# Second mixer of a two-layer decoder trunk: sums of squares of k read from the diagonal of k's product with itself instead of from transposed copies of k

## The chip, the cores and the metric

The kernel runs on 1 core of one Trainium2 chip. The metric is the device time of one execution in microseconds (us), as the median of several runs. In the profile, PE is the matmul engine (TensorE) and PEld its weight loads, DVE is VectorE, ACT is ScalarE, POOL is GpSimd and SP is the engine from whose queue most of the DMAs are issued.

## What is computed

A trunk of two layers on 512 positions of 1024 channels in float32. Layer 0 has gated linear attention as mixer, layer 1 a gated DeltaNet; each is followed by a ConvFFN, and every sublayer ends in a LayerNorm. The change lies in the DeltaNet, with 8 heads of 128 channels:

```python
def l2_normalize(x):
    return x * lax.rsqrt(jnp.sum(jnp.square(x), -1, keepdims=True) + RMS_EPS)

def gdn_mixer(x, w_in, conv_w, a_log, dt_bias, norm_w, w_out):
    proj = x @ w_in
    ...
    qkv = jax.nn.silu(causal_dwconv(qkv, conv_w))
    q, k, v = jnp.split(qkv.astype(jnp.float32), [hk, 2 * hk], axis=-1)
    qc = l2_normalize(to_head_chunks(q, GDN_HEADS, GDN_CHUNK)) * GDN_DK ** -0.5
    kc = l2_normalize(to_head_chunks(k, GDN_HEADS, GDN_CHUNK))
    ...
    o = rms_norm(gdn_chunked(qc, kc, vc, beta, gc), norm_w)
    o = from_head_chunks(o).astype(x.dtype)
    return (o * jax.nn.silu(gate)) @ w_out

def gdn_chunked(q, k, v, beta, g):
    ...
    k_beta = k * beta[..., None]
    m = jnp.where(strict, jnp.einsum('bhnik,bhnjk->bhnij', k_beta, k) * decay_ij, 0.0)
    rhs = jnp.concatenate([v * beta[..., None], k_beta * jnp.exp(bcum)[..., None]], axis=-1)
    sol = lax.linalg.triangular_solve(m, rhs, left_side=True, lower=True, unit_diagonal=True)
    ...
```

So each position's k is divided by its length, for which its sum of squares is needed, and the products of all pairs of k in a chunk, scaled by beta and a decay, form a triangular matrix that is inverted. The kernel works with blocks of 128 positions, four to a sequence, and leaves k as it comes from the convolution; the lengths enter as factors.

## The kernel before

The program is unrolled. A Python planner writes the instructions in one order, from a clock of its own (`self.clk`) that every planned matmul advances: a matmul of 128 columns in full float32 by 0.224, a transposition by 0.11, one of the wide ones (512 columns) by 0.23. Side work is written as generators that are resumed between the wide matmuls when they fall due (`spawn` with a delay, `yield` with a pause, `until` and `set` for flags). PE therefore carries out the side products at fixed places among the wide matmuls, each engine takes its instructions in the order of the program, and a late input stalls the engine at that place. The wide matmuls are the projections: `fm` (a head's channels on the partitions), then `tm` (positions on the partitions) for the gates and the output. Each fm item takes 24 wide matmuls with a split weight (high and low part, `wh` from ACT, `wl` from DVE). Four weight buffers (`WB = 4`) rotate, and when the planner takes up an item it writes the split of the item two places further on (`LOOKAHEAD = 2`).

The DeltaNet's items come in this order: k of 8 heads with the columns for beta and the decay after the fourth (`ba_done`), v of 8 heads, q of 8 heads, then the gates. `gdn_conv` takes a head's result out of PSUM (ACT, then three DVE operations, then silu on ACT).

What stands around the change:

- `squares(which, hd)` transposes a pair of heads of k or q (four 128x128 transpositions a head, tile `qkT`, one PSUM bank a head) and lets ACT square each block with an accumulator output into `ssq`.
- `k_task(hd)` is started for both heads of a pair 6.0 after the second one's conversion. It calls `squares` for the pair, waits for the flag `dt` of its head (decays ready), makes the factors `bp` and `bn` on DVE from `ssq` and beta, multiplies k with itself on PE (tile `pg`), and lets DVE scale and mask this product out of PSUM into the slot `am`. Then DMAs on the POOL and SP queues write the 32x32 diagonal blocks of `am` to DRAM (`dblk`).
- `decays` fills the tiles `dt`: 8 broadcast DMAs on POOL, transpositions (`bat`) of the tile that DVE's scan writes, DVE differences, ACT exponentials. It is started by `ba_done` and sets `dt` of head n at its end plus 0.6 n + 1.0.
- `norms(1, rk)` waits for `ssq` of all heads and makes the factors with which `v_task` scales v.
- `base` waits for `am` of all heads, loads `dblk` as `m`, inverts the 32x32 blocks with 62 dependent DVE operations, writes the result to DRAM and loads it back as `T` and `rm` for four pairs of heads. For every pair it starts `inverse`, `INV_DELAY` later by the planner's clock: four blocks of small PE products (tiles V and R) with copies on ACT and DVE between them, which build the full inverse `rm`.
- `chain(g)`, for each half of the heads, needs v, `rm` and the masked products of q and k; it runs the recurrence over the four blocks, and its last flag is `r2`. `finish` then scales the gates by the outputs, and `split_y` transposes them (`yT`) for the output projection.

SBUF slots of 128x512 float32 come from a pool of 45 in this stage (`SLOTS`), and PSUM has 8 banks.

Of the kernel before, what the change touches and what calls it, by code (L numbers as in the profile page):

```python
# [12 lines left out]
AF = mybir.ActivationFunctionType  # L13
ALU = mybir.AluOpType
# [28 lines left out]
LOOKAHEAD = 2  # L43
TAIL = 4
HEADSTART = 4
INV_DELAY = 27.0
CONV_DELAY = 6.0
COLS_DELAY = 64.0
BASE_PACE = 1.8
# [3 lines left out]
def c4(t):  # L53
    return t.rearrange("p (c i) -> p c i", c=4)


def blk(i, n=P):
    return slice(i * n, i * n + n)


class Trunk:
# [85 lines left out]
    def keep(self, shape, s, dt=F32):  # L147
        return self.cp.tile(shape, dt, name=self.uid(s), tag=s)
# [1093 lines left out]
    def gdn(self, li, g, b):  # L1242
        nc = self.nc
# [8 lines left out]
        bn, bp, rk = keep("gd_bn"), keep("gd_bp"), keep("gd_rk")  # L1252
        ssq, rr = self.own([P, 2, DH, 4], "gd_ssq"), self.own([P, DH, 4], "gd_rr")
# [3 lines left out]
        q, k, v, am, rm, pj = ([None] * DH for _ in range(6))  # L1257
# [51 lines left out]
            self.set("decays", 1.0)  # L1309


        def squares(which, hd):

            for i in (hd, hd + 1):
                pt = self.psum("qkT")
                self.tr4(pt, (q, k)[which][i])
                for ck in range(4):
                    nc.scalar.activation(pt[:, blk(ck)], pt[:, blk(ck)], AF.Square,
                                         accum_out=ssq[:, which, i, ck:ck + 1])
                self.set(("ssq", which, i))  # L1320

        def k_done(ps, hd):
            k[hd] = self.gdn_conv(ps, 8 + hd, self.resid("conv"))
            if hd % 2:
                self.spawn(k_task(hd - 1), CONV_DELAY)
                self.spawn(k_task(hd), CONV_DELAY)

        def q_done(ps, hd):
            q[hd] = self.gdn_conv(ps, hd, self.slot("conv"))
            if hd % 2:  # L1330
                self.spawn(q_task(hd - 1), CONV_DELAY)

        def k_task(hd):
            t = k[hd]
            if hd % 2 == 0:
                squares(1, hd)
            yield from self.until(("dt", hd))
            nc.vector.tensor_scalar_add(bp[:, hd, :], ssq[:, 1, hd, :], RMS_EPS)
            nc.vector.reciprocal(bp[:, hd, :], bp[:, hd, :])
            nc.vector.tensor_mul(bp[:, hd, :], bp[:, hd, :], beta(hd))  # L1340
            nc.vector.tensor_scalar_mul(bn[:, hd, :], bp[:, hd, :], -1.0)
            yield 0.5
            pg = self.psum("pg")
            self.mm4(pg, t, t)
            am[hd] = a = self.slot("am")
            for ck in range(4):
                nc.vector.scalar_tensor_tensor(a[:, blk(ck)], pg[:, blk(ck)], bn[:, hd, ck:ck + 1],
                                               pj[hd][:, blk(ck)], ALU.mult, ALU.mult)
            for qq in range(4):
                r = blk(qq, 32)  # L1350
                u = hd // 4 * 64 + qq * 16 + hd % 4 * 4
                (nc.gpsimd, nc.sync)[qq % 2].dma_start(self.dblk[u:u + 4].rearrange("c j i -> j c i"), c4(a)[r, :, r])
            self.set(("am", hd), 2.0)

        def q_task(hd):
            squares(0, hd)
            for i in (hd, hd + 1):
                yield from self.until(("am", i))
            for i in (hd, hd + 1):
                pq = self.psum("pq")  # L1360
                self.mm4(pq, k[i], q[i])
                nc.vector.tensor_mul(pj[i], pj[i], pq)

                nc.gpsimd.affine_select(c4(pj[i]), c4(pj[i]), pattern=[[0, 4], [1, P]], compare_op=ALU.is_ge,
                                        fill=0.0, base=0, channel_multiplier=-1)
                self.set(("pj", i), 2.0)
# [9 lines left out]
        def base():  # L1376
# [17 lines left out]
            for pair in range(4):  # L1394
# [6 lines left out]
                for qq in range(4):  # L1401
# [5 lines left out]
                    for i in range(2):  # L1407
                        (nc.sync, nc.gpsimd)[qq % 2].dma_start(
                            c4(rm[2 * pair + i])[rw, :, rw],
                            self.dinv[u + 4 * i:u + 4 * i + 4].rearrange("c j i -> j c i"))  # L1410
                self.spawn(inverse(pair, t8), INV_DELAY)
                yield 4.5
# [271 lines left out]
```

## Time and profile before

| | before |
|---|---|
| median of 3 runs | 1256.84 us (1256.22 to 1257.76) |
| the profiled execution | 1261.5 us, its span 1259.8 us |
| DeltaNet up to the last gate projection | about 586 to 851 us of the span |
| PE busy in the span | 1242.6 us |
| DVE busy in the span | 914.2 us |
| ACT busy in the span | 584.2 us |
| granted TensorE clock, mean | 0.997 |

A line of the groups reads: program line, engine, operation, output <- inputs, shape and count, then busy time, mean duration, and the idle time of the engine ahead of them. In the table by stretches each engine's busy time stands with the number of its instructions. The chain of waits follows the last instruction back to what released it, piece by piece.

### The profile page before, as it was taken

To read this page: it belongs to the slowest core of one execution; us is meant where nothing else is said; L and a number is where in the kernel's file an instruction comes from. 1 tells how busy PE (TensorE), PEld (TensorE's weight loads), DVE (VectorE), ACT (ScalarE), POOL (GpSimd) and SP (SyncE) were. 2 spreads that over 40 slices of the span, in tenths; PEclk is the share of its full clock that TensorE was granted. 3 is DMA by queue.
4 is the path that set the end of the run, shared out by engine and by line. 5 is a ranking of instruction groups with operands and counts; after the bars stand their busy time and mean duration, and the time that the engine had idled before them with its cause. 6 is when DMAs were issued, how large, how long until landed. Compare 5 with 4: busy or idle time off the path is not lost.

```text
span 1259.8 us, 17201 instructions
## 1 busy us (share of the span) xinstructions
PE 1242.6 (99%) x6574; PEld 1050.7 (83%) x6574; DVE 914.2 (73%) x1541; ACT 584.2 (46%) x1062; POOL 115.1 (9%) x152
## 2 busy tenths in 40 slices
PE   9999999999999999989999999999999999999997
PEld 8878888988888888879888888988988878888886
DVE  4953556689957895765689955579588966796667
ACT  4644434634434443454765544544554434443440
POOL 4000000071000000001013030010044000000000
PEclk9999999999999999999999999999999999999999
DMA  7422224342453114441344341134443173323321
GB/s 206 117 67 67 67 84 134 134 134 67 130 154 100 61 57 117 122 132 51 101 138 117 109 103 41 62 124 118 144 134 101 34 217 93 92 71 113 100 68 67
DMA packets 169410, 130.72 MB, mean 104 GB/s; under 512 B 16232, under 2 KB 139946, under 8 KB 169328
## 3 DMA queue, kind: packets, MB, share of 16 engines
q1 hardware_dynamic: 164240, 120.47, 32.2%
q0 software_dynamic: 3888, 8.50, 2.2%
q8 instruction: 51, 0.84, 0.3%
q10 hardware_dynamic: 1200, 0.66, 0.2%
q14 instruction: 31, 0.25, 0.1%
HBM read 123.82 MB, written 5.78 MB: 103 GB/s over the span
## 4 chain that ended last, share of the span: by engine, by line
PE 87%; DVE 8%; ACT 2%; DMA 2%; issue 1%; SPq 0%; DVEq 0%; ACTq 0%
PE fm L193 44%; PE tm L193 22%; PE fold L193 11%; DVE wl L571 2%; PE o L193 2%; PE xT L210 1%; DMA raw<-in_gdn_w_in_dram 1%; PE R L193 1%; DVE conv L842 1%; DVE form L842 1%; PE V L193 1%; PE qkT L210 1%; PE vn L193 1%; PE pq L193 1%; PE pg L193 1%
## 5 line engine op out<-in xcount | busy, mean ns | idle before, releaser
L193 PE MATMUL fm<-xh,wh 128*128 128x512 f32 (+2 forms) x1104 | 402.5, 367 | 0.7 <-ACT xh L571 0.7
L193 PE MATMUL fm<-xl,wh 128*128 128x512 f32 (+2 forms) x1104 | 399.9, 365 | 0.0
L193 PE MATMUL fm<-xh,wl 128*128 128x512 f32 (+1 forms) x1088 | 395.9, 366 | 0.0
L571 DVE TENSOR_TENSOR wl<-raw,wh 128x1024 fp32r<-128x1024 f32 (+1 forms) x162 | 203.0, 1255 | 195.8 <-ACT wh L571 195.6
L571 ACT CAST wh<-raw 128x1024 fp32r<-128x1024 f32 (+1 forms) x162 | 169.5, 1046 | 259.2 <-PE fm L193 155.2
L193 PEld LDWEIGHTS fm<-xh,wh 128*128 128x128 f32 (+1 forms) x1104 | 206.9, 188 | 33.8 <-ACT xh L571 0.9
L193 PEld LDWEIGHTS fm<-xl,wh 128*128 128x128 f32 (+1 forms) x1104 | 207.0, 188 | 32.7 <-DVE xl L571 0.2
L193 PEld LDWEIGHTS fm<-xh,wl 128*128 128x128 f32 x1088 | 204.2, 189 | 33.3
L193 PE MATMUL fold<-wl,fh 128*128 128x512 f32 x224 | 87.4, 390 | 1.1 <-DVE wl L571 1.1
L193 PE MATMUL fold<-wh,fh 128*128 128x512 f32 x224 | 87.6, 391 | 0.0
L193 PE MATMUL fold<-wh,fl 128*128 128x512 f32 x224 | 87.2, 389 | 0.0
L842 DVE SCALAR_TENSOR_TENSOR conv<-fm,ffn_cw,conv 128x511 f32<-128x511 f32 x112 | 83.4, 745 | 5.1 <-ACT conv L840 3.7
L193 PE MATMUL tm<-wh,xh 128*128 128x512 f32 x192 | 78.5, 409 | 0.8 <-ACT qk L1043 0.8
L571 ACT CAST wh<-b 128x1024 fp32r<-128x1024 f32 x48 | 49.6, 1053 | 59.1 <-PE fold L193 25.8
L193 PE MATMUL tm<-wh,xl 128*128 128x512 f32 x192 | 75.2, 391 | 0.0
L193 PE MATMUL tm<-wl,xh 128*128 128x512 f32 x192 | 74.9, 390 | 0.0
L860 ACT ACTIVATE conv<-conv 128x512 f32<-128x512 f32 x44 | 27.8, 632 | 81.0 <-DVE conv L842 81.0
L571 DVE TENSOR_TENSOR wl<-b,wh 128x1024 fp32r<-128x1024 f32 x48 | 57.8, 1216 | 2.3 <-ACT wh L571 2.3
L769 POOL TENSOR_TENSOR h<-h,gb 128x512 f32<-128x512 f32 x16 | 28.1, 1778 | 329.3 <-DMA gb<-in_ln_g_dram 329.3
L1237 DVE SCALAR_TENSOR_TENSOR conv<-fm,gdn_cw,conv 128x509 f32<-128x509 f32 (+2 forms) x72 | 53.2, 743 | 1.8 <-ACT conv L1235 1.0
L193 PEld LDWEIGHTS fold<-wl,fh 128*128 128x128 f32 x224 | 42.0, 188 | 10.5 <-DVE wl L571 1.9
L193 PEld LDWEIGHTS fold<-wh,fh 128*128 128x128 f32 x224 | 42.0, 188 | 9.8 <-DVE h L931 1.2
(318 smaller groups left out, 1844.4 us busy)
## 6 DMA issues: line engine op xcount, KB each, us to landing
raw<-in_ffn_w_in_dram SPq DMA_DIRECT2D x88, 512.0 KB, 3.8
raw<-in_gdn_w_in_dram SPq DMA_DIRECT2D x32, 512.0 KB, 4.1
raw<-in_ffn_w_out_dram SPq DMA_DIRECT2D x28, 512.0 KB, 3.7
b<-in_ffn_w_out_dram SPq DMA_DIRECT2D x24, 512.0 KB, 4.9
raw<-in_gla_w_in_dram SPq DMA_DIRECT2D x23, 512.0 KB, 3.7
raw<-in_gla_w_out_dram SPq DMA_DIRECT2D x8, 512.0 KB, 3.7
raw<-in_gdn_w_out_dram SPq DMA_DIRECT2D x8, 512.0 KB, 3.9
h<-in_x_dram SPq DMA_DIRECT2D x8, 256.0 KB, 5.9
```

The source lines that it names most:

```text
L193: t = self.nc.tensor.matmul(out, a, b, start=start, stop=stop, skip_group_check=joined)
L210: t = self.nc.tensor.transpose(out, a, self.ident[:n, :n])
L571: return self.nc.scalar.copy(dst_h, src), self.nc.vector.tensor_sub(dst_l, src, dst_h)
L769: nc.gpsimd.tensor_mul(h[hf], h[hf], gb[hf])
L842: nc.vector.scalar_tensor_tensor(a[:, d:], ps[:, :S - d], tap(2 - d), a[:, d:], ALU.mult, ALU.add)
L860: nc.scalar.activation(a, a, AF.Gelu)
L1237: self.conv = nc.vector.scalar_tensor_tensor(a[:, d:], ps[:, :S - d], tap(3 - d), a[:, d:], ALU.mult, ALU.add)
```

## The change

The transpositions of k and their squares on ACT go. The product of k with itself is made at the place where they stood, before the wait for `dt`. ACT copies it into the slot `am`. DVE then multiplies each of its four blocks in PSUM by the identity, in place, with a sum over the row as a second output: the diagonal, which is the sum of squares, goes to `ssq`. The pause of 0.5 behind the factors goes. The scaling and masking reads the copy in SBUF and writes it in place. `squares` serves q alone. The delay of `inverse` goes from 27 to 35.

```diff
-INV_DELAY = 27.0
+INV_DELAY = 35.0
...
-        def squares(which, hd):
+        def squares(hd):
 
             for i in (hd, hd + 1):
-                pt = self.psum("qkT")
-                self.tr4(pt, (q, k)[which][i])
+                pt = self.psum("qT")
+                self.tr4(pt, q[i])
                 for ck in range(4):
-                    nc.scalar.activation(pt[:, blk(ck)], pt[:, blk(ck)], AF.Square,
-                                         accum_out=ssq[:, which, i, ck:ck + 1])
-                self.set(("ssq", which, i))
+                    nc.scalar.activation(pt[:, blk(ck)], pt[:, blk(ck)], AF.Square, accum_out=ssq[:, 0, i, ck:ck + 1])
+                self.set(("ssq", 0, i))
...
         def k_task(hd):
             t = k[hd]
-            if hd % 2 == 0:
-                squares(1, hd)
+            pg = self.psum("pg")
+            self.mm4(pg, t, t)
+            am[hd] = a = self.slot("am")
+            nc.scalar.copy(a, pg)
+            for ck in range(4):
+                nc.vector.tensor_tensor_reduce(pg[:, blk(ck)], pg[:, blk(ck)], self.ident, 1.0, 0.0,
+                                               ALU.mult, ALU.add, ssq[:, 1, hd, ck:ck + 1])
+            self.set(("ssq", 1, hd))
             yield from self.until(("dt", hd))
             nc.vector.tensor_scalar_add(bp[:, hd, :], ssq[:, 1, hd, :], RMS_EPS)
             nc.vector.reciprocal(bp[:, hd, :], bp[:, hd, :])
             nc.vector.tensor_mul(bp[:, hd, :], bp[:, hd, :], beta(hd))
             nc.vector.tensor_scalar_mul(bn[:, hd, :], bp[:, hd, :], -1.0)
-            yield 0.5
-            pg = self.psum("pg")
-            self.mm4(pg, t, t)
-            am[hd] = a = self.slot("am")
             for ck in range(4):
-                nc.vector.scalar_tensor_tensor(a[:, blk(ck)], pg[:, blk(ck)], bn[:, hd, ck:ck + 1],
+                nc.vector.scalar_tensor_tensor(a[:, blk(ck)], a[:, blk(ck)], bn[:, hd, ck:ck + 1],
                                                pj[hd][:, blk(ck)], ALU.mult, ALU.mult)
...
         def q_task(hd):
-            squares(0, hd)
+            squares(hd)
```

## The prediction

> **What bounds the kernel now.** I read the page first: busy shares and the chain of waits.
>
> ```profile
> span 1259.8 us, 17201 instructions
> PE 1242.6 (99%) x6574; PEld 1050.7 (83%) x6574; DVE 914.2 (73%) x1541; ACT 584.2 (46%) x1062; POOL 115.1 (9%) x152
> PE 87%; DVE 8%; ACT 2%; DMA 2%; issue 1%; SPq 0%; DVEq 0%; ACTq 0%
> ```
>
> PE is never free for long, and 87% of the chain is PE. A microsecond taken from PE's list shortens the kernel by one, unless an input is then late. So I need the slack of the others around the edit: the busy times by stretches (columns: length; PE, PEld, DVE, ACT, POOL busy with counts; clock; DMA share; GB/s).
>
> ```profile
> 615.00:625.00 10.00, 10.00 (x50) 8.28 (x49) 4.76 (x12) 8.85 (x25) 0.00 (x0) 1.00 0.40 105
> 625.00:635.00 10.00, 9.60 (x45) 7.67 (x44) 9.34 (x21) 4.88 (x7) 3.45 (x7) 1.00 0.45 123
> 635.00:645.00 10.00, 10.00 (x50) 8.38 (x49) 7.30 (x16) 6.26 (x22) 1.35 (x3) 1.00 0.78 256
> 645.00:660.00 15.00, 15.00 (x81) 12.79 (x80) 14.85 (x63) 9.19 (x25) 0.00 (x0) 1.00 0.23 65
> 660.00:680.00 20.00, 20.00 (x118) 17.60 (x118) 17.78 (x54) 13.37 (x26) 11.93 (x24) 1.00 0.50 124
> 680.00:722.50 42.50, 42.50 (x213) 35.79 (x212) 41.16 (x91) 24.24 (x61) 2.91 (x6) 1.00 0.34 94
> ```
>
> PE is full in all but one stretch. DVE is nearly full from 645 to 722.5 (14.85 of 15, 17.78 of 20, 41.16 of 42.5), where it scales `am` and runs `base`. It has room only in 615 to 625 (5.24 idle) and 635 to 645 (2.70). The edit takes work from PE and gives work to DVE just ahead of DVE's full stretch; that is the whole question.
>
> **The change part by part.** (1) PE. The pieces of the chain of waits (start, length, what):
>
> ```profile
> 611.27 0.87 PE qkT L210 x8
> ...
> 616.25 0.94 PE qkT L210 x8
> ...
> 635.96 0.87 PE qkT L210 x8
> ...
> 647.74 0.87 PE qkT L210 x8
> ...
> 664.03 2.68 PE pg L193 x24
> ```
>
> The four `qkT` pieces are k's, two heads each; they go: 0.87 + 0.94 + 0.87 + 0.87 = **3.55 us** off PE. The products, 2.68 for three heads, so 0.89 a head and 7.1 in all, stay at the same price, but move to where the transpositions were.
>
> (2) ACT. It loses 32 squares with their accumulator reads and gains 8 copies of a full bank; the nearest row for a copy is the cast of `yT`.
>
> ```profile
> L1318 ACT ACTIVATE qkT<-qkT 128x128 f32<-128x128 f32 x64 | 16.7, 261 | 1.5 <-PE qkT L210 1.0
> L1318 ACT ACTIVATION_READ_ACCUMULATOR qkT<-qkT 128x1 f32 x64 | 11.9, 186 | 0.0
> L571 ACT CAST yh<-yT 128x512 fp32r<-128x512 f32 x8 | 4.3, 622 | 4.5 <-PE yT L210 4.3
> ```
>
> That is 32 x (0.261 + 0.186) = 14.3 us of durations against 8 x 0.622 = 5.0. ACT gets lighter behind a full PE: nothing on the path.
>
> (3) DVE. It gains 32 multiplications by the identity with a row sum, out of and into PSUM. No operation of DVE here writes PSUM or has an accumulator, so the price is bounded by the nearest rows: the scaling of `am` out of PSUM, and ACT's accumulator read above.
>
> ```profile
> L1347 DVE SCALAR_TENSOR_TENSOR am<-pg,gd_bn,dt 128x128 f32<-128x128 f32 x32 | 9.2, 342 | 0.0
> L1587 DVE SCALAR_TENSOR_TENSOR sg<-v,gd_r,sg 128x128 f32<-128x128 f32 x32 | 8.8, 346 | 0.0
> ```
>
> ```profile
> 669.24 2.67 DVE L1347 SCALAR_TENSOR_TENSOR am<-pg,gd_bn,dt 128x128 f32<-128x128 f32 x10
> ```
>
> Ten in a row take 2.67, so 0.267 each when they follow one another. Lower bound 0.267; upper bound a full duration and a full accumulator read, 0.342 + 0.186 = 0.528. I take 0.36, an estimate nearer the first: the streamed price with half of an accumulator read on top. In all 8.5, 11.5 or 16.9 us. Scaling `am` from SBUF instead of PSUM: 346 ns against 342, so nothing gained.
>
> [...]
>
> (4) Where DVE's extra work lands. 16 sums come after the pieces at 611 and 616, 8 after 636, 8 after 648. At 0.36 the first 5.8 us meet 5.24 us of idle time, the next 2.9 meet 2.70, the last 2.9 meet 0.15: DVE is 0.5 + 0.2 + 2.7 = **3.4 us late** at 660 (2.0 at the lower price, 3.3 + 1.5 + 4.1 = 8.9 at the upper). I credit no idle time after that, since most of it is the wait for `m`. This lateness passes to `am`, to the DMAs of `dblk`, to `m` and to the end of `base`. PE is moreover 3.55 ahead, 0.65 of an item of 5.46, and each item brings DVE three convolution steps and a `wl` (3 x 0.743 + 1.255 = 3.5 us): up to 2.3 more in front of the end of `base`.
>
> ```profile
> 684.80 10.93 PE fm L193 x48
> ...
> 731.48 1.02 PE V L193 x32
> ```
>
> ```profile
> L571 DVE TENSOR_TENSOR wl<-raw,wh 128x1024 fp32r<-128x1024 f32 (+1 forms) x162 | 203.0, 1255 | 195.8 <-ACT wh L571 195.6
> ...
> L1237 DVE SCALAR_TENSOR_TENSOR conv<-fm,gdn_cw,conv 128x509 f32<-128x509 f32 (+2 forms) x72 | 53.2, 743 | 1.8 <-ACT conv L1235 1.0
> ```
>
> (48 matmuls are two items of 24, 5.46 each.) Does a late DVE starve the wide matmuls? A split of this stretch:
>
> ```profile
> 682.37 1.05 ACT L571 CAST wh<-raw 128x1024 fp32r<-128x1024 f32 x1 [0.18 <-PE fm L193]
> ```
>
> ```profile
> 683.45 1.23 DVE L571 TENSOR_TENSOR wl<-raw,wh 128x1024 fp32r<-128x1024 f32 x1
> ```
>
> The cast starts as PE ends an item, and the split is for two items on, so due at 682.4 + 10.9 = 693.3; `wl` is there at 684.7, **8.6 us** early. Lateness of 3.4 to 5.7 stays under that. On SP's queue half of the `dblk` DMAs wait for `am`, and the next weight load waits behind them, by the same 3.4 against the same 8.6. The earlier limit is the inverse.
>
> (5) The first block of the inverse. Its last input is the third load of `T` of the first pair, issued within this row:
>
> ```profile
> 726.48 0.92 SPq L1405 DMA_DIRECT2D T<-dinvt  x2
> ```
>
> ```profile
> T<-dinvt SPq DMA_DIRECT2D x12, 32.0 KB, 2.0
> ```
>
> It lands about 727.4 + 2.0 = 729.4, and PE takes the block at 731.48: slack 2.1. Where does the block stand after the change? By the planner's sums, the last `am` flag came some 14 after the end of the decays, because eight products (0.9 of planner time each, with wide matmuls between) stood between; now it comes some 8 after, when the last `dt` flag falls due (0.6 x 7 + 1.0) plus the flag's own 2.0. The decays start 4 x 0.89 - 0.87 - 0.94 = 1.75 later. `INV_DELAY` adds 8. Sum 8 + 1.75 - 6 = +3.75; resumption only between wide matmuls makes it 3 to 5, I take 4. PE then wants the input at 735.5, and the slack is 2.1 + 4 = **6.1** against a lateness of 3.4 + 2.3 = 5.7. No stall at my price, with little to spare. With the old delay it would stall by about 8; the longer delay is part of the price.
>
> (6) The end of the stage. The chain of the second half also moves by 4:
>
> ```profile
> 836.81 0.89 PE o L193 x8
> 837.70 19.09 PE tm L193 x84
> 856.78 1.75 PE yT L210 x16
> ```
>
> ```profile
> 843.59 0.17 DVE L1575 SCALAR_TENSOR_TENSOR gd_r<-gd_rs,gd_rr 128x16 f32<-128x16 f32 x1
> ```
>
> ```profile
> 851.37 0.60 ACT L970 ACTIVATE sg<-tm 128x512 f32<-128x512 f32 x1 [0.70 <-PE tm L193]
> ```
>
> Its factors are ready at 843.76, now 847.8. The last gates, which `yT` needs as well, come 3.55 earlier: 848.4. So the gates still come last; cost 0, but the 8.2 us of cover have shrunk to 0.6.
>
> (7) The one idle place on PE:
>
> ```profile
> 629.86 0.43 PE L210 MATMUL bat<-ident,ba 64*128 64x64 f32 x4 [0.40 <-DVE ba L1274]
> ```
>
> PE arrives 1.75 later, DVE's scan is later by 0.5 (3.3 at the upper price): the 0.40 may go, or grow to 0.4 + 3.3 - 1.75 = 1.95. I take no difference. PSUM: a `pg` bank now waits for a copy and four sums instead of four squares, a microsecond or two more of one bank in eight; 0.
>
> **Sum:** -3.55 on PE, 0 elsewhere. The profiled execution took 1261.5 us around a span of 1259.8; its span would become 1256.2. It ran 4.7 us over the median of the runs, and the removed matmuls cost the same in both, so the median goes from 1256.84 to **1253.3**.
>
> **Rivals.** *A, DVE's lateness reaches PE* (slower than before). At price p the end of `base` is late by 32p - 5.24 - 2.70 - 0.15 + 2.3, and PE stands still at the first V for what exceeds 6.1. That begins at p = 0.37, eats the whole 3.55 at p = 0.48, and makes the kernel slower by 2.5 us from p = 0.56. For it: no row shows this operation, and the stretch 645 to 722.5 has no room. Against: 0.56 is above both bounds. At 0.528 the time is 1253.3 + 5.0 = 1258.3; at the price of a 512-wide step (0.743) it is 1253.3 + 11.9 = 1265.2.
>
> *B, the longer delay is what counts.* If the inverse moves by the full 8 and not by 4, the factors are ready at 851.8, after the gates at 848.4, and PE waits up to 3.4 at `yT`: 1256.7, no change. For it: only 0.6 us of cover by (6). Against: the flags of `am` do come earlier.
>
> *C, the room that the products leave also helps:* the 0.40 at `bat` goes and nothing stalls: 1252.9. Small, and inside my own range.
>
> **How the numbers follow.** Forecast (with C) 0.56, its own range 1252.2 to 1254.5; A 0.20, 1255 to 1265; B 0.20, 1255 to 1257.5; 0.04 for reorderings that I cannot work out. The range reaches from 1251.8 into A at its upper bound, with half a microsecond for the runs' own spread: 1258.8. About 0.2%, 2.5 us, can be told from no change: faster means below 1254.3, which the forecast gives but for its edge, 0.57; B and the lower part of A are within, 0.26; the rest of A is slower, 0.17.
>
> **What would show it.** PE has 32 fewer transpositions and 3.5 us less busy time in the stage. The row sum of DVE shows the price: below 0.37 a piece in succession the forecast holds; above 0.5 rival A. The first V starts near 735 without idle time ahead of it. `gd_r` of the second half ends before the last gates' silu; if `yT` waits for DVE, B. The forecast is wrong if PE shows idle time at V, at `bat` or at `yT`, or if the wide matmuls wait for `wl`.

## The result and the profile after

| | before | after |
|---|---|---|
| median | 1256.89 us (1256.22 to 1259.93) | 1259.21 us (1258.56 to 1261.94) |
| ratio after to before | | 1.0018 (95% interval 1.001 to 1.0025) |
| the profiled execution, its span | 1261.5 us, 1259.8 us | 1259.0 us, 1257.3 us |

The kernel became slower by 2.3 us, where 3.5 us less had been forecast. The page of after, its spans, busy times and chain of waits:

```profile
span 1257.3 us, 17151 instructions
PE 1241.4 (99%) x6542; PEld 1049.4 (83%) x6542; DVE 918.3 (73%) x1605; ACT 579.2 (46%) x1006; POOL 117.4 (9%) x152
PE 88%; DVE 7%; DMA 2%; ACT 1%; issue 1%; SPq 0%; DVEq 0%; ACTq 0%
```

PE has 32 instructions fewer, as meant. That this span is the shorter one says nothing: ahead of the DeltaNet the profiled execution of before waited 3.64 us for a weight tile, that of after 1.35 us (PE's timeline, before and then after):

```profile
552.75 1.22 PE L193 MATMUL tm<-fh,b 128*128 128x512 f32 x2 [3.64 <-ACT b L571]
```

```profile
550.51 0.73 PE L193 MATMUL tm<-fh,b 128*128 128x512 f32 x2 [1.35 <-ACT b L571]
```

So the stage is compared by its own length, from its first `fm` matmul to the first transposition `xT` of the LayerNorm behind it. Before:

```profile
585.82 0.28 PE L193 MATMUL fm<-xh,wh 128*128 128x256 f32 x1
...
888.34 0.93 PE L210 MATMUL xT<-ident,h 128*128 128x128 f32 x7
```

After:

```profile
582.17 0.28 PE L193 MATMUL fm<-xh,wh 128*128 128x256 f32 x1
...
886.96 1.07 PE L210 MATMUL xT<-ident,h 128*128 128x128 f32 x8 [0.24 <-DVE ln_rs L721]
```

302.52 us became 304.79: +2.27, as much as the medians lost. Each length of the stage is that of one profiled execution. What lies behind `xT` took about 370.4 us in nine of the 16 executions here and 371.1 to 371.5 in the other seven, so a time can move by 1 us without the stage. A time of after plus 3.65 (585.82 - 582.17) compares with one of before.

Where it went is at the first block of the inverse (PE's timeline of after, then busy time by stretches, PEclk third from the end):

```profile
734.37 2.21 PE L193 MATMUL V<-T,am 32*32 32x32 f32 x32 [2.45 <-DMA T<-dinvt]
736.50 1.97 PE L210 MATMUL qT<-ident,conv 128*128 128x128 f32 x8
738.26 3.19 PE L193 MATMUL pq<-conv,conv 128*128 128x128 f32 x16
```

```profile
730.00:740.00 10.00, 7.43 (x58) 6.61 (x57) 4.70 (x7) 4.95 (x19) 8.59 (x16) 0.70 0.56 120
```

PE stands idle for 2.45 us until `T` lands, and then the clock is halved: before, V took 1.09 us and `pq` 1.95 at a clock of 1.00, here 2.21 and 3.19. In steps of 0.2 us the granted clock is 1.00 up to 734.0, 2.1 us after PE stopped (734.37 - 2.45 = 731.92), and about 0.50 from there to 740.85.

Upstream is DVE (groups of after, the row sums and their accumulator reads):

```profile
L1339 DVE CUSTOM_DVE_ANT_0 pg<-pg,ident 128x128 f32<-128x128 f32 x32 | 8.6, 314 | 0.0
...
L1339 DVE DVE_READ_ACCUMULATOR2_ANT gd_ssq<- 128x1 f32 x32 | 4.5, 141 | 0.0
```

and the groups of DVE while `base` runs, in before (679.8 to 722.5) and in after (677.9 to 726.5):

```profile
L1237 DVE SCALAR_TENSOR_TENSOR conv<-fm,gdn_cw,conv 128x511 f32<-128x511 f32 (+2 forms) x21 | 15.6, 741 | 0.0
...
L571 DVE TENSOR_TENSOR wl<-raw,wh 128x1024 fp32r<-128x1024 f32 x7 | 8.5, 1221 | 0.2
L1362 DVE TENSOR_TENSOR dt<-dt,pq 128x512 f32<-128x512 f32 x2 | 1.4, 680 | 0.0
```

```profile
L1237 DVE SCALAR_TENSOR_TENSOR conv<-fm,gdn_cw,conv 128x510 f32<-128x510 f32 (+2 forms) x23 | 17.1, 743 | 0.0
L571 DVE TENSOR_TENSOR wl<-raw,wh 128x1024 fp32r<-128x1024 f32 x9 | 11.0, 1222 | 0.1
...
L1363 DVE TENSOR_TENSOR dt<-dt,pq 128x512 f32<-128x512 f32 x4 | 2.7, 681 | 0.0
```

`base` begins with the first of these lines in before and with the second in after (timeline of DVE):

```profile
679.82 0.18 DVE L1386 TENSOR_TENSOR tmp<-m,tt 128x31 f32<-128x31 f32 x1
```

```profile
677.97 0.19 DVE L1387 TENSOR_TENSOR tmp<-m,tt 128x31 f32<-128x31 f32 x1 [0.58 <-DMA m<-dblk]
```

In before's time the second is 681.62, so `base` begins 1.8 us late. Its copy into `m` ends at 726.49, which is 730.14 in before's time, against 722.49 there: 7.65 us late. The difference, 5.85 us, arises inside `base`. Its own 62 operations cost nearly the same (21.4 us against 20.9), but 5.3 us more of other work stands between them (17.1 + 11.0 + 2.7 against 15.6 + 8.5 + 1.4).

### The profile page after: what moved, and what is told of

Same layout as the page of the kernel before. It is cut to its first block, busy times and chain, and to the rows that moved or that the text cites. A ratio compares the mean times of both kernels' runs of the same rounds, so it can differ in the third digit from the quotient of the medians.

```text
span 1257.3 us, 17151 instructions
## 1 busy us (share of the span) xinstructions
PE 1241.4 (99%) x6542; PEld 1049.4 (83%) x6542; DVE 918.3 (73%) x1605; ACT 579.2 (46%) x1006; POOL 117.4 (9%) x152
## 4 chain that ended last, share of the span: by engine, by line
PE 88%; DVE 7%; DMA 2%; ACT 1%; issue 1%; SPq 0%; DVEq 0%; ACTq 0%
PE fm L193 48%; PE tm L193 19%; PE fold L193 12%; PE o L193 2%; DVE wl L571 1%; PE xT L210 1%; PE R L193 1%; PE V L193 1%; DMA raw<-in_gdn_w_in_dram 1%; PE vn L193 1%; PE pg L193 1%; DVE conv L1237 0%; PE s L193 0%; DMA h<-in_x_dram 0%; PE ks L193 0%
```

## The experiments

All kernels, with the length of the stage and the median beside the runs of before on the same chip:

| run | edit | stage, us | to before | median, us | before, us | ratio (95%) |
|---|---|---|---|---|---|---|
| after | the change | 304.79 | +2.3 | 1259.21 | 1256.89 | 1.0018 (1.001 to 1.0025) |
| e1_delay44 | delay 44 | 306.20 | +3.7 | 1260.51 | 1257.69 | 1.0024 (1.0015 to 1.0032) |
| e2_delay27 | delay 27 | 310.66 | +8.1 | 1265.09 | 1257.69 | 1.0053 (1.004 to 1.0067) |
| e3_before35 | before, delay 35 | 303.34 | +0.8 | 1258.55 | 1256.95 | 1.0008 (0.9999 to 1.0016) |
| e4_dinvt_first | `dinvt` issued first | 303.70 | +1.2 | 1259.63 | 1257.69 | 1.0015 (1.0003 to 1.0027) |
| e5_nosums | no row sums | 299.23 | -3.3 | 1254.97 | 1257.69 | 0.9976 (0.9967 to 0.9985) |
| e6_pool | sums on POOL and ACT | 301.03 | -1.5 | 1256.48 | 1256.95 | 0.9996 (0.9987 to 1.0005) |
| e7_filler | useless work ahead of V | 302.94 | +0.4 | 1258.59 | 1256.95 | 1.0013 (1.0004 to 1.0022) |
| e8_pool_y8_35 | e6, sums 8 later | 299.37 | -3.2 | 1253.94 | 1257.15 | 0.9976 (0.9968 to 0.9985) |
| e9_pool_y8_33 | the same, delay 33 | 298.72 | -3.8 | 1253.69 | 1257.15 | 0.997 (0.9958 to 0.9982) |
| e10_pool_y8_31 | the same, delay 31 | 298.40 | -4.1 | 1252.69 | 1257.15 | 0.9964 (0.9951 to 0.9977) |
| e11_pool_y5_31 | e6, sums 5 later, delay 31 | 305.87 | +3.4 | 1260.49 | 1257.16 | 1.0025 (1.0015 to 1.0035) |
| e12_delay37 | delay 37 | 301.09 | -1.4 | 1256.39 | 1257.16 | 0.9989 (0.998 to 0.9998) |
| e13_own_31 | e10, slots of their own | 298.41 | -4.1 | 1253.49 | 1257.43 | 0.9965 (0.9953 to 0.9978) |
| e13_own_33 | e9, slots of their own | 298.76 | -3.8 | 1253.27 | 1257.43 | 0.9968 (0.9956 to 0.998) |

**The delay, four ways.** The edit is one number, in the changed kernel (44, 27, 37) or in the kernel before (35):

```diff
-INV_DELAY = 35.0
+INV_DELAY = 44.0
```

> The changed kernel with INV_DELAY 44 instead of 35. Theory (the loss is the wait of the first V block for T, 2.45 us of idle time on PE ahead of it plus the low granted clock behind it): the block moves about 5 us later, T is there, no wait and no clock below 1.00 around 732 to 744; time near 1253.3. Rival 'late end' (what bounds the stage is the chain base, inverse, state chain, last factors, and the wait only moves): V comes without a wait, but yT waits some 5 us for the last sg multiplications; time 1258 to 1260.

> The changed kernel with the old INV_DELAY 27. Theory: PE asks for T about 4 us earlier (3 to 5) while T lands at the same time, so the wait at V grows from 2.45 to 6 to 7 us and the time to 1262 to 1264. Rival 'late end': the chain of the inverse starts when T lands in both, the end of the stage is where it was; time 1259, no difference.

> The changed kernel with delay 37: V stands 11 matmuls, 2.5 us, later on PE, just the length of its wait. Theory (the stall and its clock are the loss; what the delay adds at the end is under 1 us): no wait over 1 us, clock 1.00, 1255 to 1256.5. Rival 'late end' (no delay saves the sums on DVE, since base's lateness goes down the chain to yT): a wait of 1 to 3 us at yT or xT instead; 1257 to 1260.

> The kernel before with INV_DELAY 35 instead of 27 and nothing else. Theory (the delay alone is covered by the gates, as the prediction's step 6 has it): V 5 to 8 us later, last factors at 849 to 852 instead of 843.8, last gates still at 851.4, no wait at yT; the time within 0.7 us of before. Rival 'the longer delay is what costs' (the prediction's B): yT waits 2 to 4 us for sg and the clock falls behind it; 2 to 5 us slower than before.

PE's timeline with 27, with 44 and with 37:

```profile
734.79 1.79 PE L193 MATMUL V<-T,am 32*32 32x32 f32 x29 [7.96 <-DMA T<-dinvt]
```

```profile
853.38 2.05 PE L210 MATMUL yT<-ident,sg 128*128 128x128 f32 x7 [4.45 <-DVE sg L1588]
```

```profile
886.60 1.06 PE L210 MATMUL xT<-ident,h 128*128 128x128 f32 x8 [1.52 <-DVE ln_rs L721]
```

With 27 V waits 7.96 us, 1 us more than the theory had, and the time lies 1.1 us above its range; the late-end rival (no difference) falls. With 44 V does not wait, but `yT` does, for 4.45 us, and the clock falls there (to 0.50, for 6.83 us from 851.68 on): here the rival had it right, if 0.5 us too low in time. So both ends of the same chain can bind. With 37 V stands just where `T` lands and the wait at V is gone (0.1 us of idle time in 730 to 740), as the theory had it; 1.5 us of wait stand at `xT`, as the rival had it, and the kernel is 0.8 us faster than before. The change with DVE's sums can be rescued from a loss, but 2.5 of the 3.95 us that it frees on PE (3.55, and the 0.40 at `bat`) do not arrive.

The delay alone (e3) lengthened the stage by 0.8 us: `yT` does not wait, `xT` does (PE's timeline).

```profile
885.02 1.06 PE L210 MATMUL xT<-ident,h 128*128 128x128 f32 x8 [0.36 <-DVE ln_rs L721]
```

Its median is 1.6 us above before's, with an interval that reaches no change; why that is twice what its stage shows is open.

**The sums left out.** A constant takes the place of k's sums of squares:

```diff
-            for ck in range(4):
-                nc.vector.tensor_tensor_reduce(...)
+            nc.vector.tensor_scalar(ssq[:, 1, hd, :], pg[:, :4], 0.0, 200.0, op0=ALU.mult, op1=ALU.add)
```

> The changed kernel without the 32 row sums on DVE: one small operation a head (4 columns) writes the constant 200 into k's sums of squares, so the output is not the reference's. Theory (DVE's extra work makes base late): base ends 6 to 9 us earlier, T is there before PE asks for V, no wait and no low clock; time 1253 to 1254. Rival 'the sums are not it' (base is late because PE is ahead and the items bring DVE more work inside it): base ends 2 to 3 us earlier at most, some wait stays; time 1256 to 1259.

The stage is 3.29 us shorter than before, V does not wait, and the order of PE's instructions is that of the change but for V's place in one item. What a sum takes can be read off DVE's timeline in after:

```profile
611.11 0.33 DVE L1339 CUSTOM_DVE_ANT_0 pg<-pg,ident 128x128 f32<-128x128 f32 x1
611.36 0.14 DVE L1339 DVE_READ_ACCUMULATOR2_ANT gd_ssq<- 128x1 f32 x1
611.36 0.33 DVE L1339 CUSTOM_DVE_ANT_0 pg<-pg,ident 128x128 f32<-128x128 f32 x1
```

From the start of a sum to the start of the next operation, its own read not counted, it is 0.25 us where sums stand in a row and 0.21 elsewhere, 7.4 us for all 32. DVE's busy time in the same stretch of the stage, from 17.83 to 97.83 us behind its start, in after and then in this run (PE carries out 420 matmuls in both):

```profile
600.00:680.00 80.00, 80.00 (x420) 68.35 (x420) 74.16 (x248) 52.13 (x83) 16.67 (x33) 1.00 0.46 126
```

```profile
603.73:683.73 80.00, 80.00 (x420) 68.34 (x420) 68.65 (x196) 51.16 (x80) 16.67 (x33) 1.00 0.46 126
```

DVE has 5.5 us less to do there; the rest of the 7.4 shows up as other work that the sums pushed behind this stretch. The kernel pays 5.56 us for the sums (304.79 - 299.23). (The 7.9 us in the expectation of e6_pool compares stretches that begin at different places of the stage.)

In this run `base` begins here, and its copy into `m` ends at 725.00:

```profile
679.26 0.19 DVE L1385 TENSOR_TENSOR tmp<-m,tt 128x31 f32<-128x31 f32 x1 [1.12 <-DMA m<-dblk]
```

This trace has the same long wait ahead of the stage as before's (first `fm` at 585.90 and 585.82), so it compares directly. `base` begins 0.6 us earlier than in before and takes 3.1 longer, so it ends 2.4 us later without any sums. That fits PE being ahead: 24 convolution steps and 8 splits stand in it, against 21 and 7. The sums add the other 5.2 of the 7.65: 2.4 at the start of `base` and 2.8 inside it. The theory had put its gain at 6 to 9 us and the time at 1253 to 1254, so it was somewhat too high in both; the rival "the sums are not it" falls, though the first 2.4 are as it said.

The 2.8 inside `base` come with another order. After has 23 convolution steps, 9 splits and 4 `pq` products between the operations of `base`, this run 24, 8 and 2. Up to the end of `base` DVE's order is the same in after and in its runs with delays 27 and 37, with `dinvt` first and with the filler. The planner's clock counts nothing for the lines left out, so the planner wrote the rest in the same order here too; the built program need not keep it. Why it came out otherwise is not shown. What was left out is therefore the sums together with the order that came with them.

**What the stall costs.** Two useless matmuls, shortly ahead of V, all else on PE in the same order:

```diff
+            if pair == 0:
+                fill = self.psum("fill")
+                for _ in range(2):
+                    self.behind(nc.tensor.matmul(fill, self.reset[:, :P], self.reset, start=True, stop=True), self.wide)
             pv = [self.psum("V") for _ in range(2)]
```

> The changed kernel with two more matmuls on PE (128x512, f32, result unused) shortly ahead of the first V block, some 1.8 us of useless work; the order of all else on PE is the same. Theory (the stall costs its idle time and then again as much by the halved clock): T lands when it did, V starts at 734.4 as before, the idle time falls below 1 us, the clock stays at 1.00 through qT and pq; some 3 us faster than the change, 1256 to 1257. Rival 'the low clock is only a record, the stall alone costs': time unchanged at 1259, or up to 1.8 us slower.

```profile
730.39 1.88 PE L1427 MATMUL fill<-reset 128*128 128x512 f32 x4
...
734.69 0.66 PE L193 MATMUL V<-T,am 32*32 32x32 f32 x16 [1.03 <-DMA T<-dinvt]
735.52 0.66 PE L193 MATMUL V<-T,am 32*32 32x32 f32 x16 [0.17 <-DMA T<-dinvt]
736.11 1.09 PE L210 MATMUL qT<-ident,conv 128*128 128x128 f32 x8
```

```profile
730.00:740.00 10.00, 8.80 (x75) 6.82 (x73) 5.42 (x9) 5.57 (x20) 8.72 (x17) 1.00 0.62 141
```

(The profile counts each of the two as two.) V starts 0.3 us later than in after, since `T` lands later, and the clock stays at 1.00. From V's start to `xT` after needs 152.59 us and this run 150.41 (734.69 to 885.10): the halved clock cost **2.18 us**, nearly as much as the wait. This run waits 0.87 us at `xT`, after 0.24, so 0.6 us of what PE gained is lost again there. With 1.88 us of work added the stage is 1.85 us shorter. The median came down by less than expected (1258.59 for 1256 to 1257). The profiled execution had a mean granted clock of 0.999, but 8 of the 11 had 0.997 or less, against 1 of 27 of before on the same chip. So the theory is borne out by the profiled execution, and in most of the others the clock probably fell all the same; where it fell there, no trace shows.

**The queue.** `dinvt` is issued ahead of the copy into `m` and of `dinv`:

```diff
+            nc.sync.dma_start(self.dinvt.rearrange("u i c -> u (i c)"), tt)
             nc.vector.tensor_copy(m2.rearrange("p (c i) -> p c i", c=32), t3.rearrange("p i c -> p c i"))
             nc.sync.dma_start(self.dinv.rearrange("u c i -> u (c i)"), m2)
-            nc.sync.dma_start(self.dinvt.rearrange("u i c -> u (i c)"), tt)
```

> The changed kernel with the DMA of dinvt issued straight behind base's last addition, ahead of the copy into m and of dinv's DMA. Theory: T lands 1.2 to 1.6 us earlier, the wait at V shrinks from 2.45 to about 1; time 1257.7 if the granted clock still falls behind the wait, 1255.5 or less if a wait that short leaves the clock alone. If the order on the queue is worth nothing: 1259.

The source of before and of the change writes `dinv` first. In before the program that was built from it nevertheless issued `dinvt` first (timeline of SP):

```profile
721.40 0.34 SPq L1393 DMA_DIRECT2D dinvt<-tt  x1
722.51 0.34 SPq L1392 DMA_DIRECT2D dinv<-m  x1
```

In after the SP queue took `dinv` first, and a weight load just ahead of it:

```profile
724.55 0.37 SPq L281 DMA_DIRECT2D raw<-in_gdn_w_in_dram  x1
726.51 0.34 SPq L1393 DMA_DIRECT2D dinv<-m  x1
726.90 0.42 SPq L1394 DMA_DIRECT2D dinvt<-tt  x1
...
730.87 0.32 SPq L1406 DMA_DIRECT2D T<-dinvt  x1
```

With the new order `dinvt` goes at 725.63, 1.27 us earlier, and `T` still only at 730.50: `dinvt` (512 KB) took 2.7 us to land in before, 4.0 in after and 4.9 here, where the weight load and `dinv` (512 KB each) move at the same time. The DMA issues of before, after and this run (KB each, us to landing):

```profile
dinvt<-tt SPq DMA_DIRECT2D x1, 512.0 KB, 2.7
```

```profile
dinvt<-tt SPq DMA_DIRECT2D x1, 512.0 KB, 4.0
```

```profile
dinvt<-tt SPq DMA_DIRECT2D x1, 512.0 KB, 4.9
```

V starts 0.46 us earlier, not 1.2 to 1.6. A miss: the longer landing took back most of what the earlier issue gave. It fits the DMA engines being shared with the weight load: with `dinvt` first and no weight load in the 3.6 us ahead of it, it landed in 2.6 to 2.7 us (before, e5, e6, e10, e13_own_31), here, 0.7 us behind a load issued at 724.94, in 4.9. In before the next load was issued at 723.64, behind `dinvt`; that PE runs ahead of a late `base` would put it beside `dinvt`, but no run holds the load back alone.

**The sums elsewhere.** POOL selects the diagonal out of the SBUF copy and ACT sums it; DVE does neither:

```diff
+            dg = m2[:, blk(hd % 2, S)]
+            nc.gpsimd.affine_select(c4(dg), c4(a), pattern=[[0, 4], [1, P]], compare_op=ALU.is_equal,
+                                    fill=0.0, base=0, channel_multiplier=-1)
             for ck in range(4):
-                nc.vector.tensor_tensor_reduce(...)
+                nc.scalar.activation(dg[:, blk(ck)], dg[:, blk(ck)], AF.Identity,
+                                     accum_out=ssq[:, 1, hd, ck:ck + 1])
```

> The changed kernel with the diagonal taken by POOL (one select for a head, out of the SBUF copy) and summed by ACT (four accumulating copies for a head) instead of DVE; delay 35 as in the change. Theory (DVE's 7.9 us of sums are the whole cause): base is as early as in the run without sums, V does not wait, clock 1.00 there; 1254 to 1255.5, 2 to 3 us faster than before. Rival 'any late sums of squares will do it' (POOL's select and ACT's sums lengthen the way to am just as much): am later by 2 us or more, V waits again; 1257 to 1260.

V does not wait, the stage is 1.5 us shorter, the median 0.5 us lower with an interval that holds no change; the theory's 2 to 3 us did not come. What is missing stands on PE's timeline:

```profile
629.53 0.43 PE L210 MATMUL bat<-ident,ba 64*128 64x64 f32 x4 [1.49 <-DVE ba L1274]
```

ACT's sums of the second pair stand ahead of the exponentials from which DVE's scan for `bat` is made. So a pause goes in front of the sums, with three delays:

```diff
+            yield 8.0
             for ck in range(4):
                 nc.scalar.activation(dg[:, blk(ck)], dg[:, blk(ck)], AF.Identity,
```

> The POOL/ACT version with ACT's accumulating copies emitted 8 us later (so that the exponentials of ba go first on ACT), delay 35. Theory (the POOL/ACT version lost 1.5 us at bat because ACT's sums stand ahead of ba's exponentials; all else of the removed 3.55 arrives): no wait at bat, none at V; 1254.5 to 1255.5, about 1.2 us faster than the POOL/ACT version. Rival (bat was no loss, since the chain of the inverse sets the end of the stage): same as that version, 1256.5.

> The same with delay 33: V stands 6 matmuls (1.4 us) earlier on PE. Theory: T is there by 729 to 730, so no wait over 1 us, and the last factors come earlier, so the wait at xT (0.6 us) shrinks: 0.3 to 0.8 us faster than with 35. Rival (the end is not set by the delay): same as with 35.

> The same with delay 31: V stands 18 matmuls (4.1 us) earlier on PE, near 727. Theory: V waits some 2 us for T, and the clock falls or not with the length of the wait; as fast as with 35 if the clock stays, 2 us slower if it falls.

In these three the second pair of heads writes its diagonal over that of the first before it is summed, so two heads get another pair's sums. The waits at `bat` and V are gone, the stage is 3.2, 3.8 and 4.1 us shorter. With 31 a wait of 2 us at V had been expected; there is none, since with the pause `base` also ends 2.2 us earlier than in e6: `T` was issued at 721.48.

With a pause of 5 and a delay of 31 each pair is summed before its place is written again:

> The POOL/ACT version with ACT's sums 5 us later and delay 31; each head's diagonal is summed before its place in m is written again, so all sums are k's own. Theory (sums off DVE, ba's exponentials first on ACT, V no later than T needs): the stage is 3.5 to 4.2 us shorter than before; 1252.5 to 1254, faster than both kernels. Rival (the three kernels with the later sums were fast for another reason): 1256.5, as the first POOL/ACT version.

It lost everything again: V waited 3.46 us. On the SP queue of this run a weight load had got ahead of the load of `m`:

```profile
670.03 0.78 SPq L1357 DMA_DIRECT2D dblk<-am  x2
672.51 0.39 SPq L277 DMA_DIRECT2D raw<-in_gdn_w_in_dram  x1
673.44 0.34 SPq L1385 DMA_DIRECT2D m<-dblk  x1
```

`m` took 4.9 us to land (3.4 in e13_own_31, where it was issued ahead of the weight loads), and `base` began at 678.35, where it began at 674.59 in e10. So DVE's sums are one way to make `base` late, and the queue seems to be another, since here they are not on DVE; the expectation had not reckoned with the second. The last two give the second pair of heads a slot for its diagonal and keep the pause of 8, with the order of e9 and e10 on PE and SP:

```diff
-            dg = m2[:, blk(hd % 2, S)]
+            dg = m2[:, blk(hd % 2, S)] if hd % 4 < 2 else self.slot("dg")
```

> POOL's select and ACT's sums 8 us later, as in the three kernels e8 to e10, but every second pair of heads writes its diagonal to a slot of its own, so all sums are k's own; delay 31. The order on PE and SP is that of the kernel with delay 31 there. Theory (the sums on DVE took the saving; with DVE free of them and m loaded ahead of the next weights the whole 3.95 arrives): V without a wait, the stage 3.8 to 4.2 us shorter than before, 1252.5 to 1253.5. Rival (that kernel was fast because two heads had other data): 1256 or more.

> The same with delay 33. Theory: no wait at V, 1253 to 1254, some 0.5 to 1 us behind delay 31. Rival as there: 1256 or more.

```profile
671.16 0.34 SPq L1385 DMA_DIRECT2D m<-dblk  x1
...
718.77 0.34 SPq L1398 DMA_DIRECT2D dinvt<-tt  x1
...
721.47 0.50 SPq L1410 DMA_DIRECT2D T<-dinvt  x1
```

```profile
725.96 1.09 PE L193 MATMUL V<-T,am 32*32 32x32 f32 x32
```

(timelines of SP and PE with delay 31). The stage is 4.1 us shorter than before and the kernel 4 us faster than before, 0.9965 (0.9953 to 0.9978), and about 6 us faster than the change. With a delay of 33 the two figures are 3.8 and 4.2 us.

## Why the prediction was wrong, step by step

(1) The transpositions: right. Without the sums the stage is 3.29 us shorter, in the last two kernels 3.8 and 4.1, where 3.55 and the 0.40 at `bat` make 3.95.

(2) ACT: right in kind. A copy of a full bank took 0.585 us on average, where 0.622 had been read off a cast.

(3) The price of a row sum: too high. Taken at 0.36 with bounds 0.267 and 0.528, it was 0.21 to 0.25, below the lower bound. The accumulator read is an instruction of its own in the trace (32 sums, 32 reads), but the next sum starts with it: 0.14 us of duration, no time in succession.

(4) **The step that failed: where DVE's extra work lands.** The forecast let only what exceeds DVE's idle time be late, 3.4 us at its price, and added up to 2.3 us for the work that PE, being ahead, brings in front of the end of `base`: 5.7. Measured, `base` ended 7.65 us late, and less came from ahead of it than forecast: its start was 1.8 late. The term that was mis-sized is what happens inside `base`. It was put at 2.3 and was 5.85. Of that, 3.1 us stand in the run without sums too, and 2.8 came with the sums, as other work between the operations of `base`. The step had taken the order of DVE's work as given and counted only lateness. Seen by the sums, 5.2 of their 7.4 us arrived at the end of `base`, where the step's own sum at 0.25 a piece would let 1.9 through. That the lateness at the start stayed under the forecast is partly luck: the price was too high, but the credit for idle time was too high as well (the run without sums begins `base` 2.4 us earlier). DVE's idle time is time in which its next instruction waits for something (ahead of `base` for `m`: 0.58 us in after, 1.12 in the run without sums); that new work fits in only if it is ready just there is the author's reading, which no run shows alone.

(5) The first block of the inverse: PE came to V at 731.9, 735.6 in before's time, as forecast (735.5). The input did not. `dinvt` was issued 9.15 us late, 7.65 of it with `base` and the rest because it now stood behind the copy into `m` and `dinv`; it landed 1.3 us more slowly. The first load of `T` went out 10.4 us late, and the two others that V needs, which follow it more closely than in before, 8.9. Against the slack of 6.1 that leaves 2.8; the wait was 2.45. The stall was to cost its length; the halved clock behind it cost nearly as much again.

(6) The end of the stage: the times were right. In the run without sums the last factors are ready at 848.34 and the last gates' silu ends at 848.33, against 847.8 and 848.4 forecast (timelines of DVE and ACT there).

```profile
848.16 0.18 DVE L1574 SCALAR_TENSOR_TENSOR gd_r<-gd_rs,gd_rr 128x16 f32<-128x16 f32 x1
```

```profile
847.73 0.60 ACT L970 ACTIVATE sg<-tm 128x512 f32<-128x512 f32 x1 [0.70 <-PE tm L193]
```

The cost was not nothing: with the longer delay DVE does its 16 scalings after the gates instead of between them, and `xT` starts 0.8 us later (e3). That the one causes the other is likely, not shown.

(7) `bat`: the 0.40 went, as rival C had it.

So the sum that was measured: everything but the sums -3.29, the wait at V +2.45, the halved clock +2.18, together +1.34 of +2.27; the other 0.9 of what the sums cost was not taken apart. Rival A named this mechanism and its place, but let it begin at a price of 0.37 a piece; here it was there at 0.25 and less, because the lateness was put 2.9 us too low against the slack (forecast 0.4 to spare, measured 2.45 of wait). The range ended at 1258.8, 0.4 us short. Rival B's wait at `yT` came with a delay of 44 alone; at 35 and 37 the late end shows at `xT`, with 0.36 and 1.52 us.

## What to carry to other kernels

Work added to an engine that takes its instructions in order (in after PE stood 2.45 us at V, with `qT` behind it, whose inputs ACT had written by 731.55) must be followed to the chain that passes through that engine, even where its busy share leaves room: here 5.2 of 7.4 us came out at the end of `base`. Look at the order in the trace, too, since the built program need not keep the planner's. A wait of PE can cost the clock behind it, here 2.18 us on top of 2.45; useless matmuls in its place gave a shorter stage in the profiled execution, but little in the median. Where a chain of latency is tight at both ends, a delay only moves the wait from one end to the other; taking the work to engines with room (POOL, ACT) gave the saving.

## What the runs showed of the hardware

The granted clock fell 2.1 us after PE's last matmul in after (wait 2.45), and in e4 behind a wait of 2.00 with one of 0.55 close after it; it stayed at 1.00 in waits of 1.03 (e7), 1.35 (after) and 1.92 (e6). The low stretches were 3.41 us long (before, behind its wait of 3.64, and e4), 6.83 (after, e1, e11) and 13.66 (e2), so multiples of one length, 3.413 in before's clock record. By the clock records of the traces they begin 546.13 us (before), 727.04 (after), 723.63 (e2, e11), 846.51 (e1) and 730.45 (e4) behind the beginning of the first record, which is at 1.00: 160, 213, 212, 248 and 214 times 3.413. So in these six runs they begin on a grid of that length, wherever the wait lies.

DVE's multiplication with a row sum, out of PSUM and into it, was no dearer in a row than a scaling out of PSUM without one: 0.25 us from start to start against 0.26 (in before ten scalings begin at 669.24 and the next instruction at 671.82).
